# Low parts of split weights: from a subtraction on VectorE and GpSimd to a negated copy on ScalarE and an accumulating DMA

## The chip, the cores and the metric

The kernel runs on one core of a Trainium2 chip. A core has a matrix engine (TensorE, PE in the profile, with PEld for its weight loads), three engines for elementwise work (VectorE, DVE; ScalarE, ACT; GpSimd, POOL), and SyncE (SP), which here only issues transfers. Sixteen DMA engines move data between the chip's main memory and the core's on-chip memory, SBUF. The metric is device time in microseconds (us) of one execution; less is better. Before the change it is 1186.43 us, the median of three runs (1181.4, 1186.43, 1187.84).

## The reference

The program is one inference step of a two-layer decoder trunk over 576 tokens (512 of a prompt and 64 of eight short samples), all in float32.

- Layer A: RMSNorm, one product with `w_in_a` (1024 x 8192) that gives queries, forget gate, values and output gate; a gated linear recurrence over 16 heads of 128; a product with `w_out_a` (2048 x 1024); the residual.
- One shared K/V projection, `w_kv` (1024 x 512).
- Layer B: RMSNorm, a product with `w_in_b` (1024 x 4096) that gives queries and gates; sliding-window attention with 32 heads of 64 in four groups, a learned sink per head; a product with `w_out_b` (2048 x 1024); the residual and a last RMSNorm.

```python
q, fz, i, gate = jnp.split(rms_norm(x, g_norm) @ w_in, 4, axis=-1)
logf = jnp.logaddexp(jnp.log(lb), jnp.log1p(-lb) + jax.nn.log_sigmoid(fz))
k = (1.0 - lb) * jax.nn.sigmoid(-fz)
...
s = jnp.exp(b_last)[..., None] * s + jnp.einsum(
    'bhsd,bhse->bhde', kc * jnp.exp(b_last[:, :, None, :] - bc), vc)
...
o = rms_norm(o, g_onorm).reshape(b, l, D_INNER) * jax.nn.silu(gate.astype(F32))
return x + o.astype(x.dtype) @ w_out, s_new
```

The results are the two outputs `y`, the recurrence's end states, and the last 128 rows of K/V.

## The kernel before

**Split products.** TensorE reads both operands as a float32 form with a shorter mantissa (`F32R`). To keep float32 accuracy each operand is held as two tiles, high = the value rounded to that form, low = value minus high. A product is three sums over the same columns: high weight by high activation, high weight by low activation, low weight by high activation, in this order. So the low weight tile, `wlo`, is needed last. In `product` (line 227, layer A) the two token halves of 288 run side by side and `wlo` is needed after two thirds of all matmuls of the tile; in `product_cols` (line 210, K/V and layer B) the halves run one after the other, so `wlo` is first needed after a third.

**Weight tiles.** All weights pass through `split_weights`, 132 times, each time for a tile of 128 partitions by 1024 float32 (512 KB): 64 tiles of `w_in_a`, 30 of the output projections (and 2 more whose two parts go to the buffers of the activations, which are free by then), 4 of `w_kv`, 16 of queries (`bq`) and 16 of gates (`bg`). One call does this:

- line 197: SP loads `raw`, one of three buffers;
- line 199: ACT casts `raw` to `whi`, one of two buffers;
- line 203: the subtraction `wlo = raw - whi`, `wlo` being one of two buffers. `share[0]` says how many eighths of the columns DVE takes; POOL takes the others. It is 8 in layer A (`LO_A`, all on DVE), 2 for K/V (`LO_KV`: 256 columns on DVE, 768 on POOL) and 0 in layer B (`LO_B`, all on POOL).

`raw` is free again when the cast and the subtraction have read it. A slot of `whi` or `wlo` is free when the matmuls of the tile two before have read it.

**Order.** The engines run their instructions in program order, each waiting for what it needs. That order is made by a list scheduler over the tile graph: it places each instruction when a modelled engine is free, and `high_priority` raises some of them. A different instruction in one helper can thus shift rows on every engine. In layer A, heads are worked in a loop in which projections of later heads are woven between the recurrence steps of earlier ones; in layer B a list (`ORDER`, `TAIL`) sets the order of query tiles (q), gate tiles (g) and output tiles (O, o), and the attention pieces are woven between them. The time falls into the start and layer A (0 to about 640 us), its last output products and the K/V projection with the first part of layer B (640 to 760), layer B (760 to about 1140), and the last output group (to the end). The names in the trace: `wlo_a`, `wlo_o`, `wlo_kv`, `wlo_bq`, `wlo_bg` are the low tiles of the parts; `pq`, `pf`, `pi`, `pg` are the four projections of layer A; `po` an output product; `pkv`, `pbq`, `pbg` the products of the later parts; `sc`, `scs`, `pav` attention products; `kf` the scaled keys (line 1029), which `pvw` (line 1061) transposes; `u_norm_b` (line 515) layer B's normed input.

Of the kernel before, what the change touches and what calls it, by code (L numbers as in the profile page):

```python
# [10 lines left out]
F32 = mybir.dt.float32  # L11
# [4 lines left out]
AF = mybir.ActivationFunctionType  # L16
ALU = mybir.AluOpType
# [68 lines left out]
def yoco_kernel(  # L86
# [26 lines left out]
    act, dve, pool, pe, sp = nc.scalar, nc.vector, nc.gpsimd, nc.tensor, nc.sync  # L113
# [43 lines left out]
    for i in range(5):  # L157
        n = P if i < 4 else LS
# [33 lines left out]
    share = [LO_A]  # L192

    def split_weights(src, name, parts=None):
        n = src.shape[1] * src.shape[2]
        raw = wts.tile([P, 1024], F32, tag="raw", name=f"raw_{name}", bufs=3)
        sp.dma_start(raw[:, :n].rearrange("p (a c) -> p a c", a=src.shape[1]), src)
        hi, lo = parts or [wts.tile([P, 1024], F32R, tag=t, name=f"{t}_{name}") for t in ("whi", "wlo")]
        act.copy(hi[:, :n], raw[:, :n])  # L199
        c = n * share[0] // 8  # L200
        for eng, r in ((dve, slice(0, c)), (pool, slice(c, n))):
            if r.start < r.stop:
                eng.tensor_tensor(lo[:, r], raw[:, r], hi[:, r].bitcast(F32), ALU.subtract)  # L203
        return hi, lo

    def product_cols(pm, whi, wlo, x, c0, c1, width=P, w0=0, nk=KT):
# [55 lines left out]
    for i in range(5):  # L262
        n = P if i < 4 else LS
# [5 lines left out]
    for i in range(5):  # L269
        n = P if i < 4 else LS  # L270
# [7 lines left out]
        r = slice(i * P, i * P + n)  # L278
# [132 lines left out]
    def out_product(w_out, k0, ogs):  # L411

        nk = len(ogs)
        wd = 256 if nk > 2 else 512
        for mc in range(D // wd):
            src = w_out[0, k0 * P : (k0 + nk) * P, mc * wd : (mc + 1) * wd].rearrange("(k p) c -> p k c", p=P)
            whi, wlo = split_weights(src, f"o{k0}_{mc}")
            for c in range(wd // P):
                m = mc * (wd // P) + c
                pm = main(f"po{k0}_{m}")  # L420
                for _ in product(
                    pm,
                    whi,
                    wlo,
                    lambda k, j: ogs[k][0][:, j * HN : (j + 1) * HN],
                    lambda k, j: ogs[k][1][:, j * HN : (j + 1) * HN],
                    width=wd,
                    c0=c * P,
                    nk=nk,
                ):  # L430
                    pass
                h2 = s2(hT[:, m, :])
                with early():
                    dve.tensor_add(h2, h2, ps2(pm))  # L434
                yield

    def out_scaled(w_out, k0, ogs, gname, one):
# [4 lines left out]
        for mc in range(D // wd):  # L442
            src = w_out[0, k0 * P : (k0 + nk) * P, mc * wd : (mc + 1) * wd].rearrange("(k p) c -> p k c", p=P)
            whi, wlo = split_weights(src, f"o{k0}_{mc}")
            for c in range(wd // P):
                m = mc * (wd // P) + c
                pm = main(f"po{k0}_{m}")
                for _ in product(
                    pm,
                    whi,  # L450
                    wlo,
                    lambda k, j: ogs[k][0][:, j * HN : (j + 1) * HN],
                    lambda k, j: ogs[k][1][:, j * HN : (j + 1) * HN],
                    width=wd,
                    c0=c * P,
                    nk=nk,
                ):
                    pass
                h2 = hT[:, m, :]
                with tc.high_priority(offset=BOOST):  # L460
                    dve.tensor_add(s2(h2), s2(h2), ps2(pm))
                    act.activation(xhi[:, m, :], h2, AF.Copy, scale=vec(gname, m))
                    dve.scalar_tensor_tensor(
                        xlo[:, m, :], h2, vec(gname, m), xhi[:, m, :].bitcast(F32), ALU.mult, ALU.subtract
                    )
                    if m == 0:
                        act.activation(rall, h2, AF.Square)
                    else:
                        sq = one(f"nsq{m}")
                        act.activation(sq, h2, AF.Square)  # L470
                        (pool if m in SUM_POOL else dve).tensor_tensor(rall, rall, sq, ALU.add)

    def out_last(w_out, k0, ogs, each, between):


        nk = len(ogs)
        wd = 1024 // nk
        ws = []
        for mc in range(nk):
            src = w_out[0, k0 * P : (k0 + nk) * P, mc * wd : (mc + 1) * wd].rearrange("(k p) c -> p k c", p=P)  # L480
            parts = [view(x, [[1, 1024]], off=1024 * mc) for x in (xhi[:, 0, :], xlo[:, 0, :])]
            ws.append(split_weights(src, f"o{k0}_{mc}", parts))
        for j in range(2):
            for m in range(KT):
                pm = half(f"pz{k0}_{j}_{m}")
                product_half(pm, *ws[m * P // wd], lambda k: ogs[k], j, wd, m * P % wd, nk)
                h1 = hT[:, m, j * HN : (j + 1) * HN]
                with tc.high_priority(offset=BOOST):
                    dve.tensor_add(h1, h1, pm[:, :HN])
                    each(j, m)  # L490
                between(j, m)
# [32 lines left out]
    with ExitStack() as actx:  # L524
# [429 lines left out]
        for h in range(NH):  # L954
            nxt, chunks, n = {}, [], 0
# [23 lines left out]
    with ExitStack() as bctx:  # L979
# [34 lines left out]
        with tc.tile_pool(name="kvx", bufs=1) as kvx:  # L1014
# [24 lines left out]
            for c in range(4):  # L1039
# [17 lines left out]
                else:  # L1057
# [5 lines left out]
                    hi = Vc[:, :, g0 : g0 + 2, :64]  # L1063
# [509 lines left out]
```

## Time and profile before

| | before |
|---|---|
| median of three runs | 1186.43 us |
| the profiled execution's own time | 1188.2 us |
| its span | 1186.4 us |
| mean granted TensorE clock | 0.98 |
| busy PE / DVE / ACT / POOL | 1120.3 / 899.0 / 725.6 / 336.5 us |
| SP's transfers, share of 16 engines' span | 28.4% (99.14 MB) |
| the subtractions, line 203, on DVE / on POOL | 106.40 us (84) / 123.09 us (52) |
| the casts, line 199, on ACT | 138.11 us (132) |

The span is what the profile lays out; the execution's time is 1.8 us more. A busy share is an average over the whole program: what counts at a place is which wait ends last there. Rows with `L203` are the subtractions, rows with `L199` the casts, and a bracket at a row's end gives the engine's idle time ahead of it and the instruction that ended it.

### The profile page before, as it was taken

How to read it: one execution, taken by the hardware profiler on the slowest of the kernel's cores; microseconds unless marked ns; L12 is line 12 of the kernel's file. 1: busy time of each engine (PE TensorE's matmuls, PEld its weight loads, DVE VectorE, ACT ScalarE, POOL GpSimd, SP SyncE). 2: the span in 40 equal slices, each digit the busy share in tenths (PEclk: the TensorE clock that was granted, in tenths of full speed). 3: DMA queues.
4: the chain of work that ended last, by engine and by line, in shares of the span. 5: the costliest groups of instructions: out<-in, count | busy, mean ns of one | idle time of the engine just before them, and what ended most of it. 6: DMA issues, size and time to landing. Idle time of an engine off the chain costs nothing.

```text
span 1186.4 us, 27382 instructions
## 1 busy us (share of the span) xinstructions
PE 1120.3 (94%) x10967; PEld 1084.5 (91%) x10967; DVE 899.0 (76%) x2057; ACT 725.6 (61%) x1746; POOL 336.5 (28%) x306
## 2 busy tenths in 40 slices
PE   6999999999999999999999987989989989999997
PEld 5999999999898989999999987989989989998987
DVE  7888776589884597883797779567887788676786
ACT  5777774466662466761677455567746765776545
POOL 1221221121121131120122155544544453444440
PEclk9999999999999999999999998999999999999999
DMA  6343334132331423332333332211211213112202
GB/s 196 103 126 90 93 110 126 56 108 76 109 132 60 140 64 110 104 98 58 88 92 93 101 90 72 68 54 54 72 54 55 76 52 89 54 54 67 60 19 80
DMA packets 161880, 100.88 MB, mean 85 GB/s; under 512 B 3985, under 2 KB 157626, under 8 KB 161722
## 3 DMA queue, kind: packets, MB, share of 16 engines
q1 hardware_dynamic: 161754, 99.14, 28.4%
q8 instruction: 86, 1.41, 0.5%
q14 instruction: 40, 0.33, 0.1%
HBM read 86.94 MB, written 14.16 MB: 85 GB/s over the span
## 4 chain that ended last, share of the span: by engine, by line
PE 40%; DVE 13%; ACT 7%; issue 3%; POOL 1%; DVEq 0%; ACTq 0%; POOLq 0%
PE pbg L210 7%; PE po L210 5%; PE pbq L210 4%; PE po L227 4%; PE pg L227 3%; PE pf L227 3%; PE pi L227 2%; ACT P L1126 2%; PE pkv L210 2%; PE sc L1097 1%; DVE P L1101 1%; PE pq L227 1%; PE pav L1180 1%; PE pz L210 1%; DVE QS L1288 1%
## 5 line engine op out<-in xcount | busy, mean ns | idle before, releaser
L604 POOL TENSOR_TENSOR Xl<-Xl 128x72 f32<-128x72 f32 x80 | 49.6, 650 | 236.8 <-DVE Xl L601 235.5
L199 ACT CAST whi_a<-raw_a 128x1024 fp32r<-128x1024 f32 x64 | 67.2, 1050 | 65.6 <-PE po L227 35.5
L203 DVE TENSOR_TENSOR wlo_a<-raw_a,whi_a 128x1024 fp32r<-128x1024 f32 x64 | 81.4, 1277 | 32.5 <-issue 24.7
L636 POOL TENSOR_TENSOR sg<-sg,lg 128x576 f32<-128x576 f32 x16 | 26.3, 1641 | 278.2 <-ACT lg L569 278.2
L1126 ACT ACTIVATE P<-P,st 128x192 f32<-128x192 f32 (+2 forms) x128 | 54.2, 424 | 65.9 <-DVE st L1121 65.7
L1135 POOL TENSOR_SCALAR P<-P,st 128x192 f32<-128x192 f32 (+1 forms) x64 | 48.9, 773 | 109.4 <-DVE st L1128 85.3
L434 DVE TENSOR_TENSOR hT<-hT,po 128x576 f32<-128x576 f32 x32 | 24.1, 754 | 52.4 <-PE po L227 52.1
L227 PE MATMUL po<-oh,whi_o 128*128 128x288 f32 x256 | 44.5, 309 | 6.4 <-issue 2.1
L199 ACT CAST whi_o<-raw_o 128x1024 fp32r<-128x1024 f32 x30 | 31.4, 1046 | 30.7 <-PE po L227 26.2
L203 POOL TENSOR_TENSOR wlo_bg<-raw_bg,whi_bg 128x1024 fp32r<-128x1024 f32 x16 | 38.3, 2394 | 32.3 <-ACT whi_bg L199 31.1
L210 PE MATMUL po<-ohb,whi_o 128*128 128x288 f32 x224 | 43.4, 309 | 3.9 <-DVE Qs L1293 2.0
L210 PE MATMUL po<-olb,whi_o 128*128 128x288 f32 x224 | 42.3, 301 | 3.9 <-DVE olb L1395 2.0
L227 PEld LDWEIGHTS po<-oh,whi_o 128*128 128x128 f32 x256 | 37.3, 194 | 8.7 <-issue 2.3
L660 POOL TENSOR_TENSOR vb<-vst,bmask 128x512 fp32r<-128x512 f32 x32 | 36.6, 1165 | 27.3 <-DVE vst L656 14.2
L203 POOL TENSOR_TENSOR wlo_bq<-raw_bq,whi_bq 128x1024 fp32r<-128x1024 f32 x16 | 38.6, 2416 | 20.2 <-ACT whi_bq L199 20.1
L227 PE MATMUL po<-ol,whi_o 128*128 128x288 f32 x256 | 42.0, 302 | 0.0
L210 PE MATMUL pbq<-xhi,whi_bq 128*128 128x256 f32 (+1 forms) x256 | 41.4, 305 | 0.0
L227 PE MATMUL pq<-xhi,whi_a 128*128 128x288 f32 x256 | 39.5, 308 | 1.7 <-issue 1.7
L210 PE MATMUL pbg<-xhi,whi_bg 128*128 128x288 f32 x256 | 40.8, 302 | 0.3 <-ACT QS L1285 0.3
L210 PE MATMUL pbg<-xlo,whi_bg 128*128 128x288 f32 x256 | 40.8, 303 | 0.0
L210 PE MATMUL pbg<-xhi,wlo_bg 128*128 128x288 f32 x256 | 40.7, 303 | 0.0
L227 PE MATMUL po<-oh,wlo_o 128*128 128x288 f32 x256 | 40.6, 295 | 0.0
(389 smaller groups left out, 3789.7 us busy)
## 6 DMA issues: line engine op xcount, KB each, us to landing
raw_a<-in_w_in_a_dram SPq DMA_DIRECT2D x64, 512.0 KB
S<-in_state_hgrn_dram SPq DMA_DIRECT2D x32, 256.0 KB
out_dram<-S SPq DMA_DIRECT2D x32, 256.0 KB
raw_o<-in_w_out_a_dram SPq DMA_DIRECT2D x16, 512.0 KB
raw_bq<-in_w_in_b_dram SPq DMA_DIRECT2D x16, 512.0 KB
raw_bg<-in_w_in_b_dram SPq DMA_DIRECT2D x16, 512.0 KB
raw_o<-in_w_out_b_dram SPq DMA_DIRECT2D x16, 512.0 KB
xt<-in_x_prompt_dram SPq DMA_DIRECT2D x4, 512.0 KB
```

What stands on the lines that cost most here:

```text
L199: act.copy(hi[:, :n], raw[:, :n])
L203: eng.tensor_tensor(lo[:, r], raw[:, r], hi[:, r].bitcast(F32), ALU.subtract)
L210: pe.matmul(pm[:, : c1 - c0], w[:, k * width + w0 : k * width + w0 + P], x(k)[i][:, c0:c1], start=n == 0, stop=n == len(terms) - 1,)
L227: pe.matmul(pm[:, j, :HN], w[:, k * width + c0 : k * width + c0 + P], x(k, j), start=n == 0 and k == 0, stop=n == 2 and k == nk - 1,)
L434: dve.tensor_add(h2, h2, ps2(pm))
L604: pool.tensor_tensor(X8[:, :, j : j + 1], X8[:, :, j : j + 1], X8[:, :, k : k + 1], ALU.add)
L636: (pool if SGP else dve).tensor_tensor(sg, sg, l, ALU.mult)
L660: pool.tensor_tensor(t, view(vst.bitcast(F32), [[0, 4], [1, P]], off=half * P), view(bmask, [[1, 4], [0, P]]), ALU.mult,)
L1097: pe.matmul(sc[:, hf, k0[hf] :], QS[pr][:, 2 * n + hf, :], kk[:, g, ks], start=q == 0, stop=q == 1)
L1101: dve.tensor_tensor_reduce(Pt[:, pr, hf, k0[hf] :], sc[:, hf, k0[hf] :], amask[:, k0[hf] :], 0.125, NEG, ALU.add, ALU.max, accum_out=st[:, ...
L1126: act.activation(x, x, AF.Exp, bias=st[:, a : a + 1], accum_out=st[:, 8 + a : 9 + a])
L1135: (pool if e == "p" else dve).tensor_scalar(x, x, st[:, 8 + a : 9 + a], None, ALU.mult)
```

## The change

The subtraction is replaced by two instructions. ACT writes minus the high part into `wlo` (a scaled copy of `whi`). Then a transfer from SBUF to SBUF, issued on POOL's queue, adds the `raw` tile to what lies in `wlo`. The stored value is again raw minus high. `share` is still set in the program, but nothing reads it.

```diff
         act.copy(hi[:, :n], raw[:, :n])
-        c = n * share[0] // 8
-        for eng, r in ((dve, slice(0, c)), (pool, slice(c, n))):
-            if r.start < r.stop:
-                eng.tensor_tensor(lo[:, r], raw[:, r], hi[:, r].bitcast(F32), ALU.subtract)
+        act.activation(lo[:, :n], hi[:, :n].bitcast(F32), AF.Copy, scale=-1.0)
+        pool.dma_start(lo[:, :n].bitcast(F32), raw[:, :n], accum_op=ALU.add)
         return hi, lo
```

Two lines fewer: line N after 203 is line N-2 in the changed kernel; the negation is its line 200, the transfer its line 201. `raw` is now released when the transfer has read it, and the first matmul with `wlo` waits for the transfer to land.

The first place is ACT in layer B, around a query tile (`whi_bq`) at about 1067 us of the profile; `QS`, `P` and `st` are pieces of the attention, `lb` a piece of the gate's activation. Before:

```order
L199 CAST whi_bq_14068<-raw_bq_14066 128x1024
L1285 CAST QS_0_13942<-pbq_0_13950 64x4x64 x2
L1342 ACTIVATE lb_13922<-lb_13922 128x512
L1126 ACTIVATE P_0_2_13979,st_0_2_13980<-P_0_2_13979,st_0_2_13980 128x192
L1123 ACTIVATE st_0_2_13980<-st_0_2_13980 128x4
L1126 ACTIVATE P_0_2_13979,st_0_2_13980<-P_0_2_13979,st_0_2_13980 128x192 x3
L199 CAST whi_bg_14177<-raw_bg_14175 128x1024
```

The same place in the changed kernel:

```order
L199 CAST whi_bq_14185<-raw_bq_14183 128x1024
L1283 CAST QS_0_14058<-pbq_0_14067 64x4x64 x2
L1340 ACTIVATE lb_14038<-lb_14038 128x512
L200 ACTIVATE wlo_bq_14186<-whi_bq_14185 128x1024
L1124 ACTIVATE P_0_2_14096,st_0_2_14097<-P_0_2_14096,st_0_2_14097 128x192
L1121 ACTIVATE st_0_2_14097<-st_0_2_14097 128x4
L1124 ACTIVATE P_0_2_14096,st_0_2_14097<-P_0_2_14096,st_0_2_14097 128x192 x3
L199 CAST whi_bg_14295<-raw_bg_14293 128x1024
```

The negation stands behind three other ACT instructions that follow the cast, and ahead of the four exponentials of an attention piece.

The second place is POOL around the K/V tiles, about 695 to 720 us. Before:

```order
L203 TENSOR_TENSOR wlo_kv_9326<-raw_kv_9323,whi_kv_9325 128x768
L471 TENSOR_TENSOR rall<-rall,nsq_9192 128x576
L471 TENSOR_TENSOR rall<-rall,nsq_9217 128x576
L471 TENSOR_TENSOR rall<-rall,nsq_9236 128x576
L203 TENSOR_TENSOR wlo_kv_9333<-raw_kv_9330,whi_kv_9332 128x768
L1008 MEMSET vS 128x256
L1080 MEMSET Qs_9699 128x512
L1081 MEMSET pT_9701 128x256
L1080 MEMSET Qs_9700 128x512
L1081 MEMSET pT_9702 128x256
L203 TENSOR_TENSOR wlo_kv_9454<-raw_kv_9451,whi_kv_9453 128x768
```

And in the changed kernel:

```order
L201 DMA wlo_kv_9406<-raw_kv_9403 128x1024
L469 TENSOR_TENSOR rall<-rall,nsq_9316 128x576
L1006 MEMSET vS 128x256
L1078 MEMSET Qs_9779 128x512
L1079 MEMSET pT_9781 128x256
L201 DMA wlo_kv_9413<-raw_kv_9410 128x1024
L1078 MEMSET Qs_9780 128x512
L1079 MEMSET pT_9782 128x256
L201 DMA wlo_kv_9534<-raw_kv_9531 128x1024
L201 DMA wlo_kv_9541<-raw_kv_9538 128x1024
```

The issue for the second tile now stands behind three memsets that came after its subtraction before; the first tile's issue is two sums further back.

The third place is POOL at the head of layer B's first query tiles, `xlo` (line 517 before, 515 after) being the low part of the normed input. Before:

```order
L517 TENSOR_TENSOR xlo<-u_norm_b_0_9527,xhi 128x288
L517 TENSOR_TENSOR xlo<-u_norm_b_0_9535,xhi 128x288
L517 TENSOR_TENSOR xlo<-u_norm_b_0_9543,xhi 128x288
L203 TENSOR_TENSOR wlo_bq_9718<-raw_bq_9715,whi_bq_9717 128x1024
L203 TENSOR_TENSOR wlo_bq_9784<-raw_bq_9781,whi_bq_9783 128x1024
L517 TENSOR_TENSOR xlo<-u_norm_b_1_9603,xhi 128x288
L517 TENSOR_TENSOR xlo<-u_norm_b_1_9611,xhi 128x288
```

And after:

```order
L515 TENSOR_TENSOR xlo<-u_norm_b_0_9607,xhi 128x288
L515 TENSOR_TENSOR xlo<-u_norm_b_0_9615,xhi 128x288
L515 TENSOR_TENSOR xlo<-u_norm_b_0_9623,xhi 128x288
L201 DMA wlo_bq_9798<-raw_bq_9795 128x1024
L515 TENSOR_TENSOR xlo<-u_norm_b_1_9683,xhi 128x288
L515 TENSOR_TENSOR xlo<-u_norm_b_1_9691,xhi 128x288
L515 TENSOR_TENSOR xlo<-u_norm_b_1_9699,xhi 128x288
L515 TENSOR_TENSOR xlo<-u_norm_b_1_9707,xhi 128x288
L201 DMA wlo_bq_9865<-raw_bq_9862 128x1024
```

The first issue keeps its place; the second now stands behind the four `xlo` pieces of the second half.

## The prediction

> **What bounds the kernel now.** I read the page first (span, busy shares, chain of waits, queues), then the table by stage, then what TensorE waited for, then the groups of lines 199 and 203, last the timeline of single tiles.
>
> ```profile
> span 1186.4 us, 27382 instructions
> PE 1120.3 (94%) x10967; PEld 1084.5 (91%) x10967; DVE 899.0 (76%) x2057; ACT 725.6 (61%) x1746; POOL 336.5 (28%) x306
> PE 40%; DVE 13%; ACT 7%; issue 3%; POOL 1%; DVEq 0%; ACTq 0%; POOLq 0%
> q1 hardware_dynamic: 161754, 99.14, 28.4%
> ```
>
> TensorE is busy for 94% of the span and leads the chain. So work taken from DVE or POOL pays only where TensorE waits for it: 1186.4 - 1120.3 = 66 us at the very most. By stage (length, then busy time with instructions of PE, PEld, DVE, ACT, POOL, then granted clock, DMA share, GB/s):
>
> ```profile
> 0.00:40.00 40.00, 28.28 (x183) 25.75 (x184) 30.56 (x69) 24.15 (x47) 6.03 (x14) 1.00 0.61 185
> 40.00:640.00 600.00, 584.43 (x6739) 568.16 (x6738) 449.95 (x840) 365.83 (x788) 103.61 (x120) 0.99 0.33 97
> 700.00:760.00 60.00, 53.53 (x379) 52.64 (x378) 44.82 (x94) 28.21 (x66) 28.57 (x26) 0.92 0.30 86
> 760.00:1140.00 380.00, 361.23 (x2831) 350.43 (x2828) 287.66 (x880) 248.80 (x707) 178.16 (x132) 0.99 0.21 61
> ```
>
> Layer A (second row) leaves TensorE idle for 600 - 584.4 = 15.6 us, layer B (fourth) for 18.8 us. Of TensorE's waits these bear on the change (waited in all, times, longest):
>
> ```profile
> PE pvw L1061 <- DVE kf L1029: 6.3, 1, 6.3
> PE scs L1204 <- DVE Qs L1293: 5.9, 2, 3.1
> PE sc L1097 <- DVE QS L1288: 2.1, 1, 2.1
> PE po L210 <- DVE Qs L1293: 2.0, 1, 2.0
> PE po L210 <- DVE olb L1395: 2.0, 3, 1.6
> PE pav L1180 <- DVE pl L1156: 1.9, 3, 1.3
> PE pf L227 <- DVE wlo_a L203: 1.9, 3, 1.4
> PE po L210 <- DVE olb L1266: 1.8, 1, 1.8
> PE po L210 <- DVE hT L1333: 1.2, 3, 0.7
> PE pav L1180 <- DVE pk L1163: 1.2, 1, 1.2
> ```
>
> TensorE waits for a low tile for 1.9 us only. The other nine rows are DVE work of 700 us and later, 24.4 us together.
>
> **Removed: the subtractions.**
>
> ```profile
> L203 DVE TENSOR_TENSOR wlo_a<-raw_a,whi_a 128x1024 fp32r<-128x1024 f32 x64 | 81.4, 1277 | 32.5 <-issue 24.7
> L203 POOL TENSOR_TENSOR wlo_bq<-raw_bq,whi_bq 128x1024 fp32r<-128x1024 f32 x16 | 38.6, 2416 | 20.2 <-ACT whi_bq L199 20.1
> ```
>
> In layer A, DVE has 150 us of 600 idle already, so its 1.28 us per tile buys little: I book the 1.9 us of `pf`. In layer B the subtraction is on POOL, but it costs DVE time, as these rows show (start, duration, engine):
>
> ```profile
> 725.09 1.92 DVE L515 SCALAR_TENSOR_TENSOR u_norm_b<-hT,vT,rall 128x288 f32<-128x288 f32 x3
> 727.30 6.13 DVE L515 SCALAR_TENSOR_TENSOR u_norm_b<-hT,vT,rall 128x288 f32<-128x288 f32 x3
> 728.14 4.97 POOL L203 TENSOR_TENSOR wlo_bq<-raw_bq,whi_bq 128x1024 fp32r<-128x1024 f32 x2
> 735.79 0.69 PE L1061 MATMUL pvw<-ident,kf 128*128 128x128 f32 x2 [6.34 <-DVE kf L1029]
> ```
>
> Three pieces of `u_norm_b` take 1.92 us free and 6.13 us while POOL subtracts, 4.2 us more; behind them is `kf`, for which `pvw` waits 6.3 us. Without the subtraction this wait should go. The other eight waits (18.1 us) follow DVE work in a stage where POOL subtracted for much of the time; some come from the attention's own chain. I take half of them, 9 us, with ends of 0 and 18. **Gain: 1.9 + 6.3 + 9 = 17 us** (8 to 26).
>
> **Added on ACT: one negation per tile.** The nearest row is the cast of the same shape:
>
> ```profile
> L199 ACT CAST whi_a<-raw_a 128x1024 fp32r<-128x1024 f32 x64 | 67.2, 1050 | 65.6 <-PE po L227 35.5
> ```
>
> 132 x 1.05 = 139 us more, so ACT goes from 725.6 to 864 us (73%); in layer B, with its 44 subtractions after 760 us, from 248.8 to about 295 of 380 (78%). It has idle time to hold them. But ACT runs in order and the negation waits until TensorE has left the `wlo` slot; behind it stand exponentials (layer B) and `KDh` casts (K/V), for which TensorE's attention products wait. Without idle time to hide in, the whole 139 us would be paid; I take 2 us (0 to 10), since the slot is mostly free when the cast has ended.
>
> **Added: the transfer; this term decides.** No transfer from SBUF to SBUF with an addition is in this trace. The nearest is a plain load of 512 KB into idle queues at the start:
>
> ```profile
> 0.72 0.40 SPq L160 DMA_DIRECT2D xt<-in_x_prompt_dram  x1
> 4.53 1.06 ACT L266 ACTIVATE junk<-xt 128x1024 f32<-128x1024 f32 x1 [2.54 <-DMA xt<-in_x_prompt_dram]
> ```
>
> From issue to first use it took 4.53 - 0.72 = 3.8 us. Of this, one pass of the data over 16 engines is 0.284 x 1186.4 us x 0.524 / 99.14 = 1.78 us (queue row above). **Lower end: 3.8 us**, as if the addition were free. The addition reads two operands, so a second pass gives 3.8 + 1.78 = 5.6; the engines are taken by other transfers for 0.284 of the time, so on average 0.284 x 1.78 = 0.5 us of waiting more: **6.1 us, which I take**, since it is the plain load with only work added that the operation must do. **Upper end: 7.4 us**, two passes behind one whole load (5.6 + 1.78). A slower adder, or slow writing of the transfer's descriptors on POOL, is beyond this and a rival.
>
> By the Trainium skill, "DMA: Bandwidth & Descriptors", Anatomy of one DMA, a transfer issued on POOL takes about 2.0 us plus its bytes at 436 GB/s, an estimate of 3.2 us here; "Collectives: The Full Stack", The bandwidth ceiling, says that an addition halves the rate because it reads two sources, which makes it 4.4 us. No row here shows an addition. With 4.4 in place of 6.1 the sum below would be -4 us, no change that can be told.
>
> How long may it take? For each tile I took, from the timeline of before, the end of the cast and the release of the slot, let the negation (1.05 us) follow, behind the ACT rows that the new order puts ahead of it, then the issue behind the POOL rows ahead of it, and compared with the first matmul that reads `wlo`. A tile of layer A:
>
> ```profile
> 336.38 1.05 ACT L199 CAST whi_a<-raw_a 128x1024 fp32r<-128x1024 f32 x1 [0.67 <-PE pq L227]
> 336.76 2.36 PE L227 MATMUL pq<-xhi,wlo_a 128*128 128x288 f32 x16
> 354.57 2.29 PE L227 MATMUL pg<-xhi,wlo_a 128*128 128x288 f32 x16
> ```
>
> The slot is left at 339.1, the negation ends at 341.9 behind a piece of the recurrence on ACT, and `pg` needs the tile at 354.6: a lead of 12.6 us. A tight tile of layer B:
>
> ```profile
> 1066.83 1.03 ACT L199 CAST whi_bq<-raw_bq 128x1024 fp32r<-128x1024 f32 x1
> 1068.54 0.63 ACT L1342 ACTIVATE lb<-lb 128x512 f32<-128x512 f32 x1
> 1070.32 1.30 POOL L1343 TENSOR_TENSOR sgt<-sgt,lb 128x512 f32<-128x512 f32 x1
> 1074.11 1.12 PE L210 MATMUL pbq<-xhi,wlo_bq 128*128 128x256 f32 x8
> ```
>
> The negation comes behind `lb` and ends at 1070.2, the issue behind `sgt` at 1071.6, the need is at 1074.1: a lead of 2.5 us. Over 128 tiles (four at places that are written out of turn are left out) the leads are these, and the shortage at a landing time is the sum of what each lacks:
>
> | stage (tiles) | least, median lead | short at 3.8 us | at 5.6 | at 6.1 | at 7.4 | at 8 |
> |---|---|---|---|---|---|---|
> | start (5) | 3.8, 5.8 | 0 | 2.3 | 3.6 | 8.3 | 10.7 |
> | layer A (73) | 2.6, 12.4 | 1.2 | 3.3 | 5.3 | 11.7 | 17.5 |
> | K/V (7) | 3.0, 6.2 | 1.5 | 6.6 | 8.1 | 14.2 | 17.7 |
> | layer B (43) | 2.5, 8.1 | 2.5 | 14.8 | 19.8 | 37.9 | 48.7 |
> | all, us | | 5 | 27 | 37 | 72 | 95 |
>
> TensorE is the bound and runs in order, so I count each shortage in full; the stall also moves the later needs, but the later casts move with it, since slots come free later.
>
> **Moved: loads.** `raw` is held until the transfer has read it: about 2 us more for the negation and 6 for landing, less the subtraction's 1.3 to 2.4. With three buffers, and 600 / 74 = 8.1 us per tile in layer A, a buffer has 24 us for 3.8 of load, 1 of cast and about 8 behind it. SP's next load is late but not felt; POOL's other work only gains room. The added transfers raise the queues' share from 28% to between 28 + 132 x 1.78 / 1186 = 48% and 68% with two passes, not full.
>
> **Sum** at 6.1 us: +37 + 2 - 17 = **+22 us** on the span of 1186.4. The profiled execution took 1188.2 us, 1.8 above the median of 1186.43; on that median it is **1208 us**.
>
> **Rivals.**
>
> *The landing is as short as a plain load (faster).* The adding happens as the data stream by, and the time is that of the 3.8 us load: +5 + 2 - 17 = -10, so 1176 us. For it: the pass is only 1.78 of the 3.8 us, the rest is fixed, and the source is SBUF rather than main memory. Against it: two reads and the issue from POOL's queue. It decides below about 4.2 us, where the shortage is under 9 us.
>
> *The second read is half hidden (no change).* Landing at 4.2 to 5.1 us costs 9 to 20 us, which the gain cancels: about 1186 us. This is also where the rule quoted above leads.
>
> *The adder or the issue is slow (much slower).* At 8 us the sum is 95 + 2 - 17 = +80, 1266 us; at 10 us the same table gives 202, +187. Leads of layer A, 12.4 at the median, begin to go too. For it: nothing here shows how POOL writes transfers, or how fast 524 KB are added. Against it: 16 engines carry a plain load well.
>
> *DVE holds up the issue.* If POOL cannot write its descriptors while DVE works on some instructions, each issue waits for a DVE instruction, 899.0 / 2057 = 0.44 us in the mean: 6.5 us, 46 us short, 1217 us. The Trainium skill, "SBUF — State Buffer", Who interferes with whom, has such a lock for some DVE modes; no row here shows POOL issuing a transfer. I leave it inside the forecast.
>
> **How the numbers follow.** Chances: forecast (landing 5.1 to 8 us) 0.42; short landing 0.24; half hidden 0.16; slow adder 0.18. A change of under 0.5%, 6 us, can't be told in this kernel. Faster is the second case, 0.24; no change the third, 0.16; slower the first and last, 0.60. The likeliest case's own range is 1190 (5.1 us) to 1266 (8 us). The range for 8 in 10 cuts a part of both ends: from 1174, just under the short landing with its gain of 17, to 1262, just under 8 us.
>
> **What would show it.** Right: line 203 is gone; line 200 has 132 rows of about 1.05 us; transfers on a POOL queue land about 6 us after issue; TensorE's waits list `wlo_bq`, `wlo_bg`, `wlo_o` and `wlo_kv` behind a transfer, about 37 us in all, most after 700 us; `pvw`'s 6.3 us is gone; DVE and POOL lose 106 and 123 us. Wrong: waits on `wlo` under 10 us (landing short), or waits in layer A of more than 20 us (landing 8 us and more); ACT's exponentials late by the negation, seen as TensorE waiting for ACT; SP's loads of `raw` late, seen as casts waiting for a transfer.

## The result, and the profile after

The changed kernel takes 1193.91 us (median of 14 runs, 1189.78 to 1198.62) against 1185.81 us before (14 runs, 1181.4 to 1191.07): a ratio of 1.0072 with a 95% interval of 1.0057 to 1.0087. It is slower, by 8 us and not by the 22 us that were forecast. One of the four executions of e2 below was a slow one of 2138.05 us and is left out of e2's ratio.

The profiled execution of the changed kernel has a span of 1189.8 us, 3.4 us more than that of before, so a single pair of profiles shows somewhat less than the medians do. The page after (span, busy times, chain, queues):

```profile
span 1189.8 us, 27763 instructions
PE 1117.8 (94%) x10967; PEld 1082.2 (91%) x10967; DVE 749.8 (63%) x1973; ACT 838.9 (71%) x1878; POOL 321.7 (27%) x386
PE 38%; ACT 9%; DVE 7%; issue 5%; DMA 2%; POOL 1%; DVEq 0%; POOLq 0%; ACTq 0%
q0 software_dynamic: 19008, 69.21, 31.5%
q1 hardware_dynamic: 161754, 99.14, 28.5%
```

DVE lost 149 us, though its subtractions had been 106 us only: 43 us more than was taken from it. POOL lost just 15 us, since issuing the transfers now takes 0.87 us each of it. The transfers brought a queue of their own, q0, and more than doubled the load of the DMA engines. The groups and the issues of the new instructions (after the name of an issue: median us from issue to landing):

```profile
L200 ACT ACTIVATE wlo_a<-whi_a 128x1024 fp32r<-128x1024 f32 x64 | 68.0, 1063 | 5.8 <-ACT whi_a L199 4.7
L201 POOL DMA_DIRECT2D wlo_a<-raw_a x64 | 55.4, 866 | 288.0 <-ACT wlo_a L200 171.1
wlo_a<-raw_a POOLq DMA_DIRECT2D x64, 512.0 KB, 5.3
wlo_bq<-raw_bq POOLq DMA_DIRECT2D x16, 512.0 KB, 4.6
wlo_kv<-raw_kv POOLq DMA_DIRECT2D x4, 512.0 KB, 6.2
```

And TensorE's waits that are new or changed (waited in all, times, longest):

```profile
PE pkv L208 <- DMA wlo_kv<-raw_kv: 9.1, 3, 4.4
PE pa L791 <- issue: 5.4, 3, 2.1
PE po L225 <- DMA wlo_o<-raw_o: 5.1, 3, 3.5
PE po L225 <- issue: 4.0, 2, 3.4
PE pbq L208 <- DMA wlo_bq<-raw_bq: 3.7, 3, 1.5
PE scs L1202 <- DVE Qs L1291: 2.8, 2, 1.9
PE po L208 <- DMA wlo_o<-raw_o: 1.6, 3, 1.2
PE pf L225 <- DMA wlo_a<-raw_a: 0.8, 1, 0.8
```

The five rows with a DMA are the waits for the transfers, 20.3 us. The wait on the keys (`pvw`, 6.3 us before) is not in the list any more, and of the 18.1 us of other DVE waits in layer B 4.1 are left (the row of `scs`, and 1.3 us in three rows that are not shown).

Where the time went is read best by the same matmul in both profiles. The products' 6336 matmuls stand in nearly the same order in all kernels, so the time between two of them is the length of a stage. In this table each column but "forecast" is the difference from before in us, between one profiled execution of each (the third row starts with the products of layer A's last four output tiles; "b only" and the columns behind it are experiments below).

| stage | after | forecast | b only (e1) | a only (e2) | plain copy (e3) | 8 columns (e4) | a, later heads (e14) |
|---|---|---|---|---|---|---|---|
| start (first head) | +5.5 | +4 | +0.2 | +4.6 | +2.9 | +0.8 | +0.4 |
| layer A | +6.5 | +4 | -1.1 | +6.3 | -10.4 | -4.0 | -7.6 |
| last output tiles, K/V | +3.9 | +2 | -5.8 | +2.7 | -4.6 | -8.9 | +0.1 |
| layer B to the end | -12.6 | +12 | -13.1 | +0.4 | -10.4 | -12.9 | -2.0 |
| sum | +3.3 | +22 | -19.8 | +14.0 | -22.5 | -25.0 | -9.1 |

The first two rows are coarse. Seven experiments below (e1, e6, e9 to e12, e15) have the same instructions as before in them, in the same order on every engine but for a few swaps on TensorE, and their single executions still differ from before's by 0.1 to 4.6 us in the first row and by -1.2 to -7.5 in the second; most of the latter is the granted clock. The costs of places in layer A below are therefore taken from the medians and their intervals.

The forecast had most of its loss in layer B; there the changed kernel wins. What it loses, it loses before. Of layer B's 12.6 us, TensorE's idle time gives 8.3 and shorter busy time of the same matmuls 4.3.

### The profile page after: what moved, and what is told of

It is laid out like the page before. It is cut to its first block, busy times and chain, and to the rows that moved or that the text cites. A ratio compares the mean times of both kernels' runs of the same rounds, so it can differ in the third digit from the quotient of the medians.

```text
span 1189.8 us, 27763 instructions
## 1 busy us (share of the span) xinstructions
PE 1117.8 (94%) x10967; PEld 1082.2 (91%) x10967; DVE 749.8 (63%) x1973; ACT 838.9 (71%) x1878; POOL 321.7 (27%) x386
## 4 chain that ended last, share of the span: by engine, by line
PE 38%; ACT 9%; DVE 7%; issue 5%; DMA 2%; POOL 1%; DVEq 0%; POOLq 0%; ACTq 0%
PE po L208 5%; PE pbg L208 5%; PE po L225 4%; PE pbq L208 3%; PE pi L225 3%; PE pq L225 3%; PE pg L225 3%; PE pf L225 3%; ACT P L1124 2%; PE sc L1095 1%; PE pz L208 1%; PE pa L791 1%; DVE P L1099 1%; PE pav L1178 1%; DVE QS L1286 1%
## 5 line engine op out<-in xcount | busy, mean ns | idle before, releaser
L201 POOL DMA_DIRECT2D wlo_a<-raw_a x64 | 55.4, 866 | 288.0 <-ACT wlo_a L200 171.1
L200 ACT ACTIVATE wlo_a<-whi_a 128x1024 fp32r<-128x1024 f32 x64 | 68.0, 1063 | 5.8 <-ACT whi_a L199 4.7
L201 POOL DMA_DIRECT2D wlo_o<-raw_o x30 | 26.3, 875 | 145.9 <-ACT wlo_o L200 88.7
L208 PE MATMUL pbq<-xhi,wlo_bq 128*128 128x256 f32 (+1 forms) x256 | 39.9, 297 | 3.7 <-DMA wlo_bq<-raw_bq 3.7
L208 PE MATMUL po<-ohb,wlo_o 128*128 128x288 f32 x224 | 41.0, 297 | 1.6 <-DMA wlo_o<-raw_o 1.6
L225 PEld LDWEIGHTS po<-oh,wlo_o 128*128 128x128 f32 x256 | 36.9, 192 | 6.1 <-DMA wlo_o<-raw_o 6.1
L906 DVE SCALAR_TENSOR_TENSOR S<-S,E,pus 128x128 f32<-128x128 f32 x128 | 35.0, 339 | 10.9 <-PE psO L872 8.1
L225 PE MATMUL pi<-xhi,whi_a 128*128 128x288 f32 x256 | 38.8, 306 | 2.4 <-DVE KQ L559 2.4
```

Source lines behind the costliest of these rows:

```text
L200: act.activation(lo[:, :n], hi[:, :n].bitcast(F32), AF.Copy, scale=-1.0)
L201: pool.dma_start(lo[:, :n].bitcast(F32), raw[:, :n], accum_op=ALU.add)
L208: pe.matmul(pm[:, : c1 - c0], w[:, k * width + w0 : k * width + w0 + P], x(k)[i][:, c0:c1], start=n == 0, stop=n == len(terms) - 1,)
L225: pe.matmul(pm[:, j, :HN], w[:, k * width + c0 : k * width + c0 + P], x(k, j), start=n == 0 and k == 0, stop=n == 2 and k == nk - 1,)
L906: dve.scalar_tensor_tensor(S0[half][:, q, :], S0[half][:, q, :], decay(4 + bb), pus[:, q * P : (q + 1) * P], ALU.mult, ALU.add,)
```

## The experiments

All ratios are to the kernel before, run on the same chip, with 95% intervals.

### One half of the program at a time

`e1_add_in_b` has the negation and the transfer only in layer B, `e2_add_in_a` only in layer A:

```diff
+        if share[0] == LO_B:        # e2: LO_A
             act.activation(lo[:, :n], hi[:, :n].bitcast(F32), AF.Copy, scale=-1.0)
             pool.dma_start(lo[:, :n].bitcast(F32), raw[:, :n], accum_op=ALU.add)
+        else:
+            ... the subtraction as before
```

> Negation and accumulating transfer only in layer B (from the first query tile on); layer A and K/V keep the subtraction. Theory: the change loses about 16 us before layer B and wins back about 13 us in it, since POOL no longer holds DVE up there. Then this kernel is faster than before by 10 to 18 us: ratio to before 0.985 to 0.992. Rival: layer B only catches up because everything before it was late (loads and casts had more time), so there is nothing to win by itself: ratio 0.997 to 1.003.

> Negation and accumulating transfer only in layer A, from the start to its last output tile; K/V and layer B keep the subtraction. Theory: the loss of the start and of layer A, about 12 us, stands alone: ratio 1.007 to 1.013. Rival, that lateness at the end of layer A is caught up in layer B whatever its low tiles are made with: ratio 1.000 to 1.003.

Measured: e1 0.9861 (0.9828 to 0.9894), 1168.51 us; e2 1.0155 (1.0116 to 1.0195), 1204.76 us. The two add up to 1.0016. The K/V tiles, which neither has, give 1.0057 alone (e11, below), and the three together 1.0073, within the intervals the whole change. So the result is the difference of a gain of about 17 us and a loss of about 25. Layer B's gain stands without a late layer A, and layer A's loss is larger than its theory said.

### What the addition costs

`e3_plain_copy` copies `raw` over the low tile without adding; `e4_one_column` adds 8 of the 1024 columns. Both leave out part of the low tile's value, so they only give a time:

```diff
-        pool.dma_start(lo[:, :n].bitcast(F32), raw[:, :n], accum_op=ALU.add)
+        pool.dma_start(lo[:, :n].bitcast(F32), raw[:, :n])                       # e3
+        pool.dma_start(lo[:, :8].bitcast(F32), raw[:, :8], accum_op=ALU.add)     # e4
```

> The changed kernel with a plain transfer in place of the accumulating one: raw is copied over the low tile, so the low part is left out of the result; all instructions, waits and bytes written are as in the change. It prices the addition. Theory: a packet takes about half as long (the change's added packets take 0.33 us each, other packets of 4 KB in the trace before 0.16), the landing is about 1.3 us shorter, and TensorE's 20 us of waits on landing fall to 6 to 10: ratio to before 0.993 to 0.998. Rival, that the fixed part of the transfer and ACT's negation make the loss: ratio 1.004 to 1.008, as the change.

> The changed kernel with the accumulating transfer cut to the first 8 of 1024 columns: the addition of the rest is left out. Issue, waits and negation stay, the moving of data goes. Theory: the landing falls to its fixed part, about 2 us, nothing is left for TensorE to wait for, and what remains is the negation on ACT: ratio to before 0.985 to 0.992 if that is nearly free, as layer B makes believe. Rival, that ACT's 140 us are the loss: ratio 1.000 or more.

Measured: e3 0.9832 (0.9795 to 0.9869), 1166.54 us; e4 0.9817 (0.9778 to 0.9855), 1163.99 us. The issues of e3 (median us to landing last):

```profile
wlo_a<-raw_a POOLq DMA_DIRECT2D x64, 512.0 KB, 3.8
wlo_bq<-raw_bq POOLq DMA_DIRECT2D x16, 512.0 KB, 3.0
```

Both are faster than their theories said (0.993 and 0.985 at best). A plain copy of the tile lands 1.5 to 1.6 us sooner than an adding one (5.3 and 4.6). Leaving out the addition is worth 27 us in all; with it goes a part of the DMA engines' load (0.67 to 0.50 of their time in layer A, 40 to 640 us). By the trace's packets, the 16,896 packets of 4096 bytes take 339 ns each (median) with the addition and 160 ns without; an engine has 8 of them per tile, 2.7 us against 1.3. The Trainium skill, "Collectives: The Full Stack", The bandwidth ceiling, has an addition at half the rate because of its two reads: the packets agree, by a factor of 2.1. The estimate of 4.4 us that the prediction worked out from this and set aside is near layer B's 4.6.

In e4 the negation, the issue and the waits are all there and only the data are gone. It is 22 us under the kernel before all the same, so ACT's 132 negations of 1.06 us cost little: what costs in the change is the transfer's data.

### Why layer B gains

`e9_b_dead_subtract` is e1 with, besides, the old subtraction on POOL into a scratch tile that nothing reads; `e10_b_dead_memset` has memsets there instead:

```diff
             pool.dma_start(lo[:, :n].bitcast(F32), raw[:, :n], accum_op=ALU.add)
+            for c in range(0, n, 512):                                           # e9
+                pool.tensor_tensor(dump[0], raw[:, c : c + 512], hi[:, c : c + 512].bitcast(F32), ALU.subtract)
+            for m in (512,) * 4:                                                 # e10
+                pool.memset(dump[0], 0.0)
```

> The kernel with the transfer in layer B only (e1_add_in_b), and besides it, behind each transfer's issue, the old subtraction on POOL into a scratch tile that nothing reads, in two halves. Theory: the gain in layer B came from DVE no longer being held up by POOL's subtraction. Then it is lost again though no one waits for these results: DVE's busy time rises by about 35 us over that kernel's 856.6 us, and the ratio to before is 0.994 to 1.002. Rival: the gain came from something else (low tiles ready sooner): 0.985 to 0.989, as e1_add_in_b.

> The same with memsets on POOL of about the same busy time (four of 128 x 512, about 2.1 us for a tile) in place of the dead subtraction: POOL's queue is as full, but POOL reads nothing. Theory, that it is the reading of operands that holds DVE: the gain stays, ratio 0.985 to 0.990. Rival, that a full POOL queue delays POOL's own attention work: ratio as e9_b_dead_subtract, 0.994 to 1.002.

Measured: e9 1.0 (0.9974 to 1.0026), 1187.17 us; e10 0.9971 (0.9945 to 0.9996), 1183.36 us. The dead subtraction takes the whole gain back: from the first K/V product to the end, e1's profiled execution is 18 us shorter than before's and e9's 1 us longer. One place is that of the prediction, the wait on the keys. In e9 three pieces of `u_norm_b` and the `xlo` piece behind them run while POOL subtracts (the last row is from TensorE's waits):

```profile
726.57 3.97 DVE L522 SCALAR_TENSOR_TENSOR u_norm_b<-hT,vT,rall 128x288 f32<-128x288 f32 x3
730.46 5.07 DVE L524 TENSOR_TENSOR xlo<-u_norm_b,xhi 128x288 fp32r<-128x288 f32 x1
PE pvw L1068 <- DVE kf L1036: 8.0, 1, 8.0
```

In e10, where POOL writes memsets between its pieces there:

```profile
726.28 1.93 DVE L522 SCALAR_TENSOR_TENSOR u_norm_b<-hT,vT,rall 128x288 f32<-128x288 f32 x3
PE pvw L1068 <- DVE kf L1036: 3.4, 1, 3.4
```

Beside the memsets the three pieces take as long as they took free, 1.92 us. In e1 the wait is 1.4 us. So POOL's subtraction does hold DVE up there, and POOL's memsets do not. The same shows in two groups of DVE in layer B (760 to 1140 us; busy time, mean ns of one). Before:

```profile
L1191 DVE TENSOR_TENSOR sgt<-ao,sgt 128x256 f32<-128x256 f32 x29 | 28.0, 965 | 2.5 <-POOL sgt L1343 2.0
L1121 DVE SCALAR_TENSOR_TENSOR st<-st,nsnk 128x4 f32<-128x4 f32 x29 | 17.1, 590 | 0.9
```

In e1, without POOL's subtraction:

```profile
L1195 DVE TENSOR_TENSOR sgt<-ao,sgt 128x256 f32<-128x256 f32 x32 | 14.9, 467 | 0.9 <-POOL sgt L1347 0.5
L1125 DVE SCALAR_TENSOR_TENSOR st<-st,nsnk 128x4 f32<-128x4 f32 x30 | 6.1, 203 | 0.9
```

In e9, with a dead one:

```profile
L1198 DVE TENSOR_TENSOR sgt<-ao,sgt 128x256 f32<-128x256 f32 x29 | 17.9, 617 | 0.8 <-POOL sgt L1350 0.4
L1128 DVE SCALAR_TENSOR_TENSOR st<-st,nsnk 128x4 f32<-128x4 f32 x29 | 9.3, 320 | 0.9
```

A DVE instruction on 128 x 4 elements takes 203 ns on average in e1, where POOL subtracts nothing in layer B, and 590 ns before. DVE's busy time over the program is 899.0 us before, 856.6 in e1 and 885.5 in e9. Of the nine waits on DVE of the prediction TensorE has 24.4 us before, 5.8 in e1 and 15.3 in e9. So these waits are about half of what e9 loses; the clock is the other half: from the K/V products on, the time taken off by a granted clock under 1 is 6.5 us in e1 and 16.2 in e9.

e10's ratio is in the range of its rival, but it did not test in layer B what it was made for. Its memsets depend on nothing, and the scheduler put them all early, the last at 825 us (POOL's memsets, stretch by stretch: length, busy time, clock, DMA share, GB/s):

```profile
700.00:760.00 60.00, 37.26 (x68) 0.91 0.43 104
760.00:880.00 120.00, 46.71 (x86) 0.99 0.48 110
880.00:1000.00 120.00, 0.00 (x0) 1.00 0.56 128
```

Its loss against e1 is in the stages up to 880 us (18 us), where TensorE waits 10.9 us for `wlo_bq`, 3.7 in e1: the memsets stand ahead of the issues on POOL's queue. From there on its stages are those of e1. What it does say is that 104 us of memsets on POOL (84 of them in the first two rows) leave DVE's busy time alone: 858.0 us, 856.6 in e1, where e9's 127 us of subtraction added 29. That agrees with the Trainium skill, "SBUF — State Buffer", Who interferes with whom: a DVE instruction with two inputs in SBUF contends with a POOL instruction that reads there, not with one that only writes. And it shows that a full POOL queue is a loss of its own kind once transfers are issued from it.

`e6_lo_b_dve` takes the other way out: no transfer, layer B's subtraction on DVE.

```diff
-LO_B = 0
+LO_B = 8
```

> The kernel before with layer B's subtraction moved from POOL to DVE (all eight eighths), no negation and no transfer. It frees POOL as the transfer does, and it ends DVE being held up by POOL's subtraction, but DVE gets 46 subtractions of about 1.25 us, 58 us, on top. Theory, that the 40 us by which DVE was held up were the loss: DVE's busy time is about 18 us over before, and the ratio 0.995 to 1.010. Rival, that a free POOL makes the gain: ratio 0.986 to 0.992.

Measured: 0.9898 (0.9872 to 0.9924), 1176.75 us. DVE's busy time is 903.4 us, 4 more than before, with 48 more subtractions of about 1.25 us. So POOL's subtractions had held DVE up for about 56 us, and doing them on DVE itself takes hardly more of its time than having POOL do them. The ratio misses the theory's range (0.995 at best) and lies in the rival's, a free POOL. e6 frees POOL and ends the holding up at once, so it can't tell the two apart. By the medians 12 of e1's 17 us are to be had with no transfer. The profile supports less: of the 13 us by which e6's execution is shorter, 7 lie in the first two rows of the table, where its instructions are those of before, and 6 from the first K/V product on. The wait on the keys falls there from 6.3 to 2.8 us, but of the 18.1 us of other DVE waits 14.4 stay, where e1 has 4.4. In e1 neither engine subtracts in layer B.

### Where the loss before layer B lies

`e11_add_in_kv` has the transfer for the four K/V tiles alone.

```diff
+        if share[0] == LO_KV:
```

> Negation and accumulating transfer only for the four K/V tiles, all else as before. In the changed kernel TensorE waits 9.1 us for them. Theory, the leads there are too short by themselves (3 to 6 us): the same waits come, the clock dips behind the two long ones, and with the later wait on the keys unchanged the ratio is 1.004 to 1.011. Rival, that the landing was late there because layer A's transfers filled the queues: ratio 0.999 to 1.003.

Measured: 1.0057 (1.0037 to 1.0078), 1192.7 us. The waits come by themselves, 8.3 us with a median landing of 6.2 us, so layer A's transfers are not needed for them. And a wait costs more than its length, as this piece of TensorE's timeline in e11 shows (start, duration, eight matmuls each):

```profile
702.54 1.21 PE L214 MATMUL pkv<-xlo,whi_kv 128*128 128x288 f32 x8
707.65 2.29 PE L214 MATMUL pkv<-xhi,wlo_kv 128*128 128x288 f32 x8 [3.90 <-DMA wlo_kv<-raw_kv]
709.74 1.70 PE L214 MATMUL pkv<-xhi,whi_kv 128*128 128x288 f32 x8
711.28 1.23 PE L214 MATMUL pkv<-xlo,whi_kv 128*128 128x288 f32 x8
```

Behind 3.9 us of waiting, 16 matmuls take 3.6 us to be started where they take 2.1 else, another 1.5 us lost. The Trainium skill, "TensorE: Matmul & The Clock Gate", Part 1, has a clock that is halved after an idle window of about 3.4 us and for as long. Half the pace agrees (2.1 us for the first eight, 1.06 is usual), and so does the length: in the clock records of all runs here, every slow stretch but the last of each program is at half for 3.4 us or two or three times that, a loss of 1.7 us at a time. The length of the wait does not agree: in the profile before, behind the start, seven of the nine waits of 1.7 to 3.1 us are followed by four microseconds with a mean granted clock of 0.57 to 0.77. Whether idle time shortly ahead of them counts too was not tried.

In layer A, three kernels have the transfer for the `w_in_a` tiles from the second head on, and besides: for nothing else (e14), for the output tiles (e17), for the first head (e18).

```diff
+        if share[0] == LO_A and name[0] == "a" and name[:3] != "a0_":    # e14
+        if share[0] == LO_A and name[:3] != "a0_":                       # e17
+        if share[0] == LO_A and name[0] == "a":                          # e18
```

> The kernel with the transfer in layer A only (e2_add_in_a, ratio 1.0155), but with the old subtraction for the first head's four tiles and for all output tiles, so 60 tiles of the later heads are left on the transfer, with leads of mostly over 10 us. Theory, that the loss sits where leads are short: most of it goes, ratio 1.000 to 1.006. Rival, that it is spread over layer A (fuller queues, code fetched late, ACT): 1.009 or more.

> The kernel with the transfer in layer A only (e2_add_in_a, ratio 1.0155), the first head's four tiles on the old subtraction. Theory, that the start and the output tiles each carry about half of the loss: ratio 1.005 to 1.012. Rival, that the output tiles carry it all: 1.013 or more; or that the start does: 0.997 to 1.002.

> The same kernel with the output tiles of layer A on the old subtraction and the first head's on the transfer. Theory, half each: ratio 1.000 to 1.008. Rival, that the output tiles carry all of the loss: 0.995 to 1.000; or none: 1.012 or more.

Measured: e14 0.997 (0.9947 to 0.9992), 1183.71 us; e17 1.0141 (1.011 to 1.0173), 1202.9 us; e18 1.0042 (1.0019 to 1.0064), 1191.82 us. Where leads are long the transfer costs nothing and may be a small gain (3.6 us; the theory had 1.000 at best). By the ratios the first head costs about 8 us over e14 and the 16 output tiles about 20. The two do not add up, though: with the output tiles on the transfer already, the first head costs only 2 us more (e2 against e17), and with the first head the output tiles 13 (e2 against e18). So the output tiles carry more than half. e17 by itself met its rival, that they carry it all, and not its theory; e18 met its theory, half each, and its rivals fell.

But for the output tiles TensorE waits 5.6 us in e17. The rest of the 20 is other idle time and slow clock: the whole run's granted clock is 0.974 in e17 and 0.986 in e14. The longest wait in e17, and POOL's two issues there with their landing (350 to 372 us):

```profile
368.95 2.29 PE L231 MATMUL po<-oh,wlo_o 128*128 128x288 f32 x8 [3.80 <-DMA wlo_o<-raw_o]
371.04 2.12 PE L231 MATMUL po<-oh,whi_o 128*128 128x288 f32 x8
372.95 2.12 PE L231 MATMUL po<-ol,whi_o 128*128 128x288 f32 x8
374.88 1.29 PE L231 MATMUL po<-oh,wlo_o 128*128 128x288 f32 x8
```

```profile
L202 POOL DMA_DIRECT2D wlo_o<-raw_o x2: 852/853/854, 358.9 to 363.8; - x2
DMA to landing us min/median/max: 8.4/9.2/10.0
```

The landing takes 10 us here, not 4.5. SP had issued a copy of 1920 KB from one place of main memory to another 7 us before, two stores of states 2 us before and a load of `raw_o` just then. Three kernels with that copy two heads earlier test the collision: the change (e19), the kernel before (e20), and e17 (e21).

```diff
-CACHE = 7
+CACHE = 5
```

> The changed kernel with the 1920 KB copy issued in the sixth head instead of the eighth (CACHE 5 for 7). Theory, that its collision with the output tiles' transfers makes the 3.5 us wait and the slow clock behind it: ratio to before 0.997 to 1.003 where the change has 1.007. Rival, that the tiles are late without it: 1.006 or more.

> Control: the kernel before with the copy issued in the sixth head. In it TensorE waits for no transfer there, so both theories expect no change: ratio 0.997 to 1.003.

> The kernel with the transfer in layer A but for the first head (e17_a_all_but_first, 1.0141), with the copy issued in the sixth head. Theory, that the collision carries most of the output tiles' loss: ratio 1.000 to 1.008. Rival: 1.011 or more.

Measured: e19 1.0052 (1.0031 to 1.0072), 1191.62 us; e20 1.0006 (0.9993 to 1.002), 1186.73 us; e21 1.0096 (1.007 to 1.0122), 1197.68 us. Both theories miss, and neither rival is met; the control is as expected. By stages (kernels with the same layer A differ by some 3 us in a quarter), the quarter of layer A from which the copy went gets shorter, by 13.4 us in e19, 15.1 in e21, and 9.7 in the control; the quarter that it went to gets longer, by 12.1, 9.3 and 6.7. So the copy costs some 7 to 10 us wherever it stands, and without the change too, where another load seems to come late (in e20 TensorE waits 5.6 us on a state behind it); the change adds a few us to that. The collision is there, but it carries about 5 of the output tiles' 20 us (1.0141 to 1.0096), and not the rest.

`e13_early` raises the two new instructions in the scheduler's order, in the whole change, `e12_b_early` in e1:

```diff
+        with early():
             act.activation(lo[:, :n], hi[:, :n].bitcast(F32), AF.Copy, scale=-1.0)
             pool.dma_start(lo[:, :n].bitcast(F32), raw[:, :n], accum_op=ALU.add)
```

> The changed kernel with both new instructions raised in the scheduler's order, so that the negation stands nearer to its cast on ACT. Theory, that the loss before layer B is late issue: TensorE's 20 us of waits on landing halve, ratio to before 0.995 to 1.003. Rival, that ACT's other work, now behind the negations, is late in its place, or that the slot's release sets the issue: ratio 1.005 or more.

> The kernel with the transfer in layer B only (e1_add_in_b), the two new instructions raised in the scheduler's order. TensorE still waits 5.5 us for low tiles there. Theory, that these come from late issue: they shrink, ratio 0.980 to 0.986. Rival, that what is raised pushes back the attention's exponentials on ACT: ratio 0.986 to 0.992.

Measured: e13 1.0072 (1.0047 to 1.0097), 1194.86 us; e12 0.984 (0.9823 to 0.9858), 1170.83 us. No gain in the whole change, whose waits for transfers stay at 19.0 us (20.3): the order of the two is not what makes its tiles late. e12 is in its theory's range and its waits for low tiles go from 5.5 to 3.9 us, but it is not faster than e1 beyond the intervals. A third buffer for the low tile, which would let the negation start before TensorE has left the old one, was not tried.

A part of layer A's loss is in the rows "issue", gaps of TensorE that end with no releaser in the trace. They sum to 11.2 us in the changed kernel and 6.0 before, and they sort the kernels in two: 8.5 to 12.8 us in the nine that add whole tiles in layer A, 4.1 to 6.4 in the eleven others, the plain copy (4.9) and the eight columns (5.9) among them. In each such gap over 1 us that I looked at (before, after, e2 and e3) a packet of 16 KB on the DMA queue for instructions ends 1.2 to 1.6 us before TensorE goes on. So the adding transfers seem to make TensorE's instructions come late, some 5 us in all; that they are what TensorE waits for is read from the times alone and was not tried by itself.

Of the output tiles' 20 us, 5.6 us are waits for the transfers, 2 us "issue" (12.7 in e17, 10.5 in e14), and 9 us are the same matmuls taking longer in layer A. The granted clock accounts for these: the time lost to it up to the first K/V product is 11.9 us in e17 and 1.7 in e14. What stays open is how much of this lost clock the transfers cause, since in the kernels with before's layer A it is 1.7 to 9.2 us, and the waits for the output tiles are only three.

### Versions that beat both

`e15_add_in_b_kv_dve` is e1 with the K/V subtraction on DVE; `e16_later_heads_and_b` has the transfer for layer B and layer A's later heads as well.

```diff
-LO_KV = 2
+LO_KV = 8
...
+        if share[0] == LO_B:                                                    # e15
+        if share[0] == LO_B or name[0] == "a" and name[:3] != "a0_":            # e16
```

> The kernel with the transfer in layer B only (e1_add_in_b), and the K/V tiles' subtraction wholly on DVE, so that POOL subtracts nowhere. If POOL's K/V subtractions hold DVE up too (a quarter tile takes DVE 1.7 us there where a whole one takes 1.25 elsewhere), 2 to 5 us more are won: ratio 0.981 to 0.985. Rival: nothing waits there, 0.986.

> The transfer where leads are long: layer A's w_in_a tiles from the second head on, and layer B; the first head, layer A's output tiles and the K/V tiles keep the subtraction, all of it on DVE. Theory, that the two gains (0.997 and 0.983 alone) add: ratio 0.977 to 0.983. Rival, that they do not, since layer A's is made up by waits elsewhere: 0.983 to 0.988.

Measured: e15 0.9832 (0.9812 to 0.9851), 1169.54 us; e16 0.9814 (0.9769 to 0.9858), 1164.42 us, the fastest kernel that computes the whole reference, 22 us under before. It leaves the transfer out where leads are short (first head, output tiles of layer A, K/V) and has POOL subtract nowhere. The gain over e1 is inside the intervals, so whether layer A's share adds is not settled.

## Why the prediction was right and wrong

- **The bound** was read right: TensorE stays at 94%, and what moved the time did so through its idle time and the slow clock that goes with it.
- **The direction** was right, the size not: +8 us for +22. And the sum hides that its places were wrong. Layer A alone was forecast at about +8 us with the start and came out at +18 (e2); layer B with the keys' wait was forecast at about +5 and came out at -17 (e1); the K/V tiles at +8 and at +7 (e11). Layer A's loss was too small by 10 us and layer B's had the wrong sign, so that the sum still came out slower, and inside the range of its likeliest case, is partly luck.
- **The landing, 6.1 us**, is the mis-sized term. It is 4.6 in layer B, 5.3 in layer A, 6.2 in K/V, and TensorE's waits for it are 20 us instead of 37: K/V 9.1 (8.1 forecast), start and layer A 5.9 (8.9), layer B 5.3 (19.8 forecast). The step that failed is the base of 3.8 us, with 0.5 us of queueing on top at every place. The load that it was read from is the program's first transfer: in its packets (4 KB each, like the tile's) seven of the first eight take 1.1 to 1.3 us, where the median is 0.16. A tile copied inside SBUF without addition lands in 3.0 us where queues are quiet (e3). Why the first packets are slow no run shows. The second pass was sized well, 1.78 us for 1.6, though by a queue whose packets are mostly of 512 bytes. The 0.5 us of queueing is about right as an average in layer A (0.7) and wrong as a constant: the landing is 4.5 us at its shortest and 9.7 at its longest, and what costs is the longest.
- **The gain, 17 us**, is the other. The choice of half for the 18.1 us of DVE waits in layer B was too cautious: 14 of them went. POOL's subtraction held DVE up for 42 us (e1 against before) to 56 us (e6) over the program, and not for the 4.2 us of the quoted place alone; that it kept all of the 14 us waiting is not shown, since the dead subtraction in e9 brings back only 3 of them, and the wait on the keys in full. The trace had the holding up: a 128 x 4 instruction on DVE with a mean of 590 ns there and a shortest of 143. Also not in the sum was that a wait that goes takes a stretch of slow clock with it (the same matmuls are 4.3 us shorter in layer B).
- **Each wait counted at its length.** A wait costs more, since the slow clock comes behind it: the 3.9 us for K/V cost 5.4 (e11). So the waits that came and those that went were both put too low.
- **The leads** were worked out well: with the landings as measured, the prediction's own table gives about 21 us of waits (an estimate between its columns: start and layer A 5, K/V 9, layer B 8), and 20.3 were measured. But it goes by one landing for all tiles. At about 359 us the transfer takes 9.7 us beside the 1920 KB copy. I took how long a landing is on average, and not which transfers run beside the tiles with short leads.
- **Not in the sum**: the "issue" gaps, 5 us more; and POOL's time to issue, 132 times 0.87 us, 115 us. POOL was to lose 123 us and lost 15. What that costs in the change was not tried; a full POOL queue ahead of the issues cost 18 us in e10.
- **ACT's negation** was right: 1.06 us each (1.05 forecast) and near free, by e4. ACT's busy time rose by 113 us to 838.9, not to 864.
- **The loads moved later** were right: SP waits for the transfers now, and TensorE waits for a high tile no longer than before (1.9 us, once).
- **Rivals**: a landing as short as a plain load's was wrong by 0.8 us in layer B; e3, which lands in 3.0 to 3.8 us, shows a gain there, of 20 us. The half-hidden second read had the right landing for layer B, 4.6 us being inside its 4.2 to 5.1, but not for layer A and K/V (5.3 and 6.2 us), and its time of about 1186 us did not come. The slow adder: 2.1 times a plain packet's time, no more than the second read. DVE holding up POOL's issue: an issue takes 0.85 to 1.04 us, nothing shows it.

## What to carry to other kernels

Before moving work off an engine, look at what the work does to the engine beside it: a short instruction whose mean is three times its shortest is being held up, and moving the culprit can pay more than its own busy time (here 60 us of subtractions moved onto the very engine that they held up added only 4 us to it). An extra transfer is priced by its packets and by what runs at the same time, not by the first load of the program, so use it tile by tile: where the lead is well over the longest landing, and not where it is near the shortest. And when a sum of a gain and a loss comes out near nothing, run each part alone; here the parts were -17, +18 and +7 us.

## What was not expected of the hardware

- An accumulating transfer inside SBUF takes 339 ns per 4 KB packet, a plain one 160 ns; a 512 KB tile lands in 4.5 us at the least, a plain copy in 2.8, and 8 columns of it in 2.0 to 2.2.
- Most waits of TensorE of 1.7 us and more are followed by 3.4 us at half the clock (eight matmuls in 2.29 us above, 1.21 before the wait).
- A DVE instruction on 128 x 4 elements took up to 1695 ns in the kernel where POOL subtracts; 104 us of memsets on POOL left DVE's busy time as it was.
- The nine kernels with whole adding transfers in layer A have 8.5 to 12.8 us of gaps of TensorE with no releaser in the trace, the eleven others 4.1 to 6.4.
